# Expert bias loads in a transformer kernel: their own tiles in the first block's pool, on SyncE's queue behind the first weights of the output projection, and the down biases by GpSimd

## The chip, the cores and the metric

The kernel runs on one core of a Trainium2 chip. The time is device microseconds of one execution, and the time before is the median of three runs: 1835.69 us (1834.64 to 1837.01). The profile is one more execution, of 1836.42 us, whose instructions span 1834.6 us.

## The reference, cut to what matters

The program is a stack of two transformer blocks for 256 tokens of width 1024 (256 more tokens serve as context), all in float32. The first block ends in a mixture of 32 experts, the second in a plain network. The part around the change is the end of the first block's attention, the router, and the experts, which have biases on all three projections:

```python
mix_x = jnp.concatenate([att_x, four_x], axis=-1) @ w_out[l]
x = x + g1 * rms_norm(mix_x, norm_attn_post[l])
hx2 = modulate(x, norm_ffn_pre[l], sh2, sc2)
# moe(hx2): the router picks 4 of 32 experts for each token
logits = jnp.dot(h, w_router) + b_router
top_logit, top_idx = lax.top_k(logits, TOP_K)
...
g = jnp.minimum(xb @ w_gate[e] + b_gate[e], SWIGLU_LIMIT)
u = jnp.clip(xb @ w_up[e] + b_up[e], -SWIGLU_LIMIT, SWIGLU_LIMIT)
act = g * jax.nn.sigmoid(SWIGLU_ALPHA * g) * (u + 1)
return act @ w_down[e] + b_down[e]
```

The biases `b_gate`, `b_up` and `b_down` are 32 rows of 1024 numbers each. The weights of each expert are 12 MB, 384 MB for all of them.

## The kernel before

**Stages.** The first block is written as `pre_project` (modulation and the input projection), `pre_attend` (attention), `pre_finish` (the rest of the output projection, the residual, the router's logits and the first ranks), `route` and `experts`. The second block follows. Instructions stand in each engine's queue in the order in which the code issues them, and each queue is worked off in that order.

**The weight stream.** All large weights come through one list of jobs (`Stream`), 1 MB a tile, issued by SyncE's queue (SP) at line 161 into five rings of buffers of 7, 6, 3, 2 and 3 tiles. `pump` issues the next job as soon as its ring has a free place in the program's order; on the chip the issue waits for the buffer's last reader. Some jobs carry small loads that are issued with them (the table `also`, line 394). For the output projection four tiles `w_out` come in the order 3, 0, 1, 2; ACT and DVE split each into a high and a low part (lines 1564 and 1565) that live in ring 1, which then serves the first tiles of the experts. The 21 first expert tiles fill all five rings: expert 0's gate and up, expert 1's gate (8 + 4 tiles), expert 1's up (4), expert 0's down (4) and one tile more. Ring 3 opens when the attention's pool closes, ring 4 when all of `pre_finish` is done.

**Semaphores of the transfers.** Transfers issued by SP and ACT signal on eight semaphores, DMAHW0 to DMAHW7, one for each transfer in turn. Before a semaphore is used again the issuing queue waits for the transfer that used it last. The waits stand in the order shown below in brackets.

**The end of the output projection.** `out_part(i)` (line 361 for its matmuls) adds part i of eight to four banks: token tile 0 in banks 0 and 1, token tile 1 in banks 2 and 3. Its last call issues parts 6 and 7 bank after bank, six matmuls each. After each call one small job of the list `fills` (line 866) is issued: the gain row, the router's bias and weights, the bias rows of the second block (line 1695), then `expert_bias_in`, which issues eight loads from ACT's queue (`b_gate` and `b_up` in two halves each, lines 957, and `b_down` in four pieces, line 960), and `bias_split`, in which ACT casts the raw biases (line 968) and DVE subtracts (line 971). The raw tiles `braw` take over two places of the pool B, by the tags `mrow` and `uT`; `mrow` holds the second block's bias table until then, and `uT` a part of the keys.

**The tail.** `gained` squares the two banks of a token tile on ACT (line 888) and scales them on DVE (line 890); `added` makes the root mean square and adds to `x` (lines 894 to 899); `turned` transposes `x` on TensorE (line 905) and copies it (line 906), and `logits` multiplies by the router's weights (line 916). An Exp table is loaded (line 928), the ranks are made (lines 1007 and 1008) and the expert stage begins with the gather of tokens (line 1291) and the first gate matmul (line 1208). `warm` issues matmuls whose results nobody reads.

Of the kernel before, what the change touches and what calls it, by code (L numbers as in the profile page):

```python
# [9 lines left out]
F32 = mybir.dt.float32  # L10
# [9 lines left out]
P = 128  # L20
D = 1024
KD = 8
T = 256
E = 32
# [15 lines left out]
QMOD, KVA, SMALL, QA, EARLY = 1, 3, 0, 2, 3  # L40
# [178 lines left out]
class Kernel:  # L219
# [143 lines left out]
    def pre_project(self, A, B):  # L363
        tc, nc, I = self.tc, self.nc, self.I
# [7 lines left out]
        for nm, n in rows:  # L372
            src = I[nm]
            if len(src.shape) == 2:
# [15 lines left out]
        kp = lambda a: a.rearrange("(k p) f -> p k f", p=P)  # L390
# [1 line left out]
        nc.sync.dma_start(out=x, in_=tp(I["x"][0]))  # L392
        nc.sync.dma_start(out=xc, in_=tp(I["ctx"][0]))
        also = {("i", 3): [(pc, I["pre"]), (self.wf, I["w_fourier"][0].rearrange("(i g) c d -> (g c) i d", g=2))],
                ("q", 2): [(self.wr, kp(I["w_router"][0])), (self.br, I["b_router"])], ("k", SMALL): self.post_small()}

        def add(nm, q, cols, f, split=None):
            st.add(cols, lambda v: f(v) + also.get((nm, q), []), 0, split)
# [1 line left out]
        for q in range(4):  # L400
            for i in (1, 0):
                o = D * i + 256 * q
# [49 lines left out]
        b = self.bank()  # L452
# [77 lines left out]
        for k in range(KD):  # L530
            if k % 2 == 0:
                w = st.get()
            h = (hi[k // 4][:, k % 4], lo[k // 2][:, k % 2])
# [15 lines left out]
            else:  # L549
                st.prepare(EARLY)  # L550
                b = self.bank("vr", "m")
# [298 lines left out]
    def pre_finish(self, B, C, R):  # L850

        nc, st = self.nc, self.stream
        mod, bo = self.mod, self.bo
        gu = B.tile([P, 2048], F32, tag="sqk", name="gu")
        g1b = gu[:, 0:D]

        def router():

            b = self.bank("lb", "s")
            for k in range(KD):  # L860
                nc.tensor.matmul(b[:, 0:E], mod[:, 0, 24 + k : 25 + k].to_broadcast([P, P]), self.wr[:, k], start=(k == 0), stop=False)
            nc.tensor.matmul(b[:, 0:E], self.c("ones", 1), self.br, start=False, stop=True)
            nc.vector.tensor_copy(self.lbias, b[:, 0:E])
            nc.vector.tensor_tensor(self.wr, self.wr, self.a2.unsqueeze(2).to_broadcast([P, KD, E]), OP.mult)

        fills = [lambda: self.bcast_row(C, self.gc, g1b, bank="b"), router, lambda: self.bias_rows(B), lambda: self.expert_bias_in(B, R),
                 lambda: self.bias_split(R)]

        for i in range(2, KD):
            self.out_part(i)  # L870
            if fills:
                fills.pop(0)()

        x, ident = self.x, self.c("ident")
        ss = C.tile([P, 2], F32, name="ss2")

        self.sd = R.tile([P, 2], F32, name="sd")
        self.r2 = R.tile([P, 2], F32, name="r2")
        xT = B.tile([P, 2048], F32, tag="pc", name="x1T").rearrange("p (k t) -> p k t", k=KD)
        self.logits = {}  # L880

        s2 = [C.tile([P, 4], F32, name=f"s2{t}") for t in range(2)]
        us = {}

        def gained(t):
            for n in range(2):
                jk = C.tile([P, 512], F32, tag="prob", name="jk", bufs=3)
                nc.scalar.activation(jk, bo[2 * t + n], AF.Square, accum_out=s2[t][:, n : n + 1])
                u = us[t, n] = B.tile([P, 512], F32, tag=("mrow", "uT")[n], name="u") if t else gu[:, D + 512 * n : D + 512 * n + 512]
                nc.vector.tensor_tensor(u, bo[2 * t + n], g1b[:, 512 * n : 512 * n + 512], OP.mult)  # L890

        def added(t):
            s = s2[t]
            nc.vector.tensor_tensor(s[:, 2:3], s[:, 0:1], s[:, 1:2], OP.add)
            nc.scalar.activation(s[:, 3:4], s[:, 2:3], AF.Sqrt, bias=self.eps[1e-6], scale=1.0 / D)
            nc.vector.reciprocal(s[:, 3:4], s[:, 3:4])
            for n in range(2):
                o = x[:, t, 512 * n : 512 * n + 512]
                nc.vector.scalar_tensor_tensor(o, us[t, n], s[:, 3:4], o, OP.mult, OP.add)

        def turned(t):
            for h in range(2):
                b = self.bank()
                for k in range(4):
                    nc.tensor.transpose(b[:, k * P : (k + 1) * P], x[:, t, (4 * h + k) * P : (4 * h + k + 1) * P], ident)
                nc.scalar.copy(xT[:, 4 * h : 4 * h + 4, t * P : (t + 1) * P], b.rearrange("p (k t) -> p k t", k=4))

        def norm(t):
            r = self.sd[:, t : t + 1]
            nc.scalar.activation(gu[:, 0:D] if t else B.tile([P, D], F32, tag="lk0", name="jk2"), x[:, t], AF.Square, accum_out=ss[:, t : t + 1])  # L910
            nc.scalar.activation(r, ss[:, t : t + 1], AF.Sqrt, bias=self.eps[1e-6], scale=1.0 / D)

        def logits(t):
            self.logits[t] = self.bank("lb", "o")[:, 0:E]
            for k in range(KD):
                nc.tensor.matmul(self.logits[t], xT[:, k, t * P : (t + 1) * P], self.wr[:, k], start=(k == 0), stop=(k == KD - 1))

        self.route_open(R)
        gained(0)
        added(0)  # L920
        gained(1)
        turned(0)
        added(1)
        norm(0)
        logits(0)
        turned(1)
        norm(1)
        nc.scalar.activation(ss[:, 0:1], self.eps[1e-6], AF.Exp)
        self.choose(0)
        logits(1)  # L930
        self.ranks_of(0)
        self.choose(1)
        self.warm(WARM2)
        self.ranks_of(1)
        self.warm(WARM3)
        self.dump("x1", x)
# [9 lines left out]
            self.moe_end(M)  # L946
        self.held.close()

    def expert_bias_in(self, B, R):


        self.braw = {}
        for nm, tag in (("b_gate", "mrow"), ("b_up", "uT")):
            t = self.braw[nm] = B.tile([P, 512], F32, tag=tag, name="braw")
            b = self.I[nm]
            for h in range(2):
                self.nc.scalar.dma_start(out=t[64 * h : 64 * h + 64], in_=bass.AP(tensor=b.tensor, offset=b.offset + 512 * h, ap=[[0, 2], [D, E], [1, 512]]))
        self.bdn = R.tile([P, T], F32, name="bdn")
        for q in range(4):
            self.nc.scalar.dma_start(out=self.bdn[E * q : E * q + E], in_=self.I["b_down"][0][:, T * q : T * q + T])  # L960

    def bias_split(self, R):

# [1542 lines left out]
```

## Time and profile before

| what | value |
|---|---|
| median of three runs | 1835.69 us |
| the profiled execution | 1836.42 us, span 1834.6 us |
| TensorE busy, share of the span | 1732.3 us, 94% |
| VectorE / ScalarE / GpSimd busy | 752.9 / 589.9 / 57.9 us |
| bytes moved | 553.45 MB, mean 302 GB/s |
| mean granted TensorE clock | 0.983 of full |

The page draws the span in 40 slices of 45.9 us. In slices 7 to 25 (from 275 us to 1147 us) the transfers run at 410 to 413 GB/s: that is the expert stage. Before it the rates lie between 197 and 405 GB/s, and the granted clock is below 9 tenths in the third and the fifth slice: these stages are made of short steps that wait for each other. After it the second block has TensorE busy in 9 tenths of nearly every slice and the transfers at 23 to 249 GB/s. Times in the text are microseconds from the span's start.

### The profile page before, as it was taken

The numbers are of one execution on the slowest core, as the hardware profiler recorded it, in microseconds if no ns is written. First come the engines' busy times: TensorE is split into PE (matmuls) and PEld (weight loads), VectorE is DVE, ScalarE is ACT, GpSimd is POOL, SyncE is SP. The second block draws the span as 40 slices with busy tenths as digits, with TensorE's granted clock in tenths as the row PEclk, the third lists the DMA queues.
The fourth block names the chain that finished last, engine by engine and source line by source line (L and its number), as shares of the span: only waits on it lengthen the run. The fifth ranks groups of instructions, "written<-read, shape, count | busy, mean of one in ns | idle before, by whom it ended". The sixth has DMA issues, their size and how long they took to land. (4 is left out here: it accounts for less than half of the span.)

```text
span 1834.6 us, 24464 instructions
## 1 busy us (share of the span) xinstructions
PE 1732.3 (94%) x9537; PEld 1038.8 (57%) x9537; DVE 752.9 (41%) x1582; ACT 589.9 (32%) x1158; POOL 57.9 (3%) x52
## 2 busy tenths in 40 slices
PE   7889599999999989999989988899999999999998
PEld 6756553333333323333323332388689989989997
DVE  4786242222222212222211211476675558756555
ACT  4544221111111101111111110355654445555444
POOL 0340000000000000000000000100000001000000
PEclk9989799999999999999999999999999999999999
DMA  9767599999999999999999999987245554435540
GB/s 350 262 242 265 197 356 405 412 412 411 410 412 413 412 412 412 410 411 412 412 413 412 413 411 411 338 249 230 70 161 186 185 188 154 132 116 203 185 158 23
DMA packets 202525, 553.45 MB, mean 302 GB/s; under 512 B 11136, under 2 KB 87558, under 8 KB 200358
## 3 DMA queue, kind: packets, MB, share of 16 engines
q1 hardware_dynamic: 201026, 549.82, 79.4%
q8 instruction: 76, 1.25, 0.3%
q10 hardware_dynamic: 932, 1.29, 0.2%
q0 software_dynamic: 448, 0.73, 0.1%
q14 instruction: 43, 0.35, 0.1%
HBM read 550.71 MB, written 1.07 MB: 301 GB/s over the span
## 5 line engine op out<-in xcount | busy, mean ns | idle before, releaser
L1565 DVE TENSOR_TENSOR ring<-ring,ring 128x1024 fp32r<-128x1024 f32 x196 | 230.6, 1221 | 78.2 <-ACT ring L1564 77.6
L1208 PE MATMUL g<-ring,xg 128*64 128x512 f32 x1056 | 254.0, 603 | 8.1 <-DMA ring<-in_w_gate 8.1
L1208 PE MATMUL u<-ring,xg 128*64 128x512 f32 x1056 | 248.2, 602 | 10.7 <-DMA ring<-in_w_up 9.7
L1219 PE MATMUL y<-ring,ht 128*64 128x512 f32 x1056 | 241.1, 599 | 15.9 <-DMA ring<-in_w_down 15.4
L1564 ACT CAST ring<-ring 128x1024 fp32r<-128x1024 f32 x196 | 195.3, 1049 | 75.7 <-PE acc L1794 54.3
L1280 ACT ACTIVATE z<-y,gsl 64x512 fp32r<-64x512 f32 x66 | 45.0, 682 | 428.6 <-PE y L1219 401.6
L1779 PE MATMUL ot<-ahi,ring 128*128 128x256 f32 x960 | 177.2, 282 | 0.0
L1219 PEld LDWEIGHTS y<-ring,ht 128*64 128x64 f32 x1056 | 69.9, 136 | 164.6 <-issue 117.6
L1281 DVE SCALAR_TENSOR_TENSOR z<-y,gsl,z 64x512 fp32r<-64x512 f32 x66 | 49.5, 750 | 250.6 <-ACT z L1280 250.5
L1779 PEld LDWEIGHTS ot<-ahi,ring 128*128 128x128 f32 x960 | 151.3, 191 | 1.3
L1208 PEld LDWEIGHTS u<-ring,xg 128*64 128x64 f32 x1056 | 67.3, 136 | 132.5 <-issue 98.9
L1208 PEld LDWEIGHTS g<-ring,xg 128*64 128x64 f32 x1056 | 66.9, 136 | 126.9 <-issue 118.7
L1779 PE MATMUL ot<-alo,ring 128*128 128x256 f32 x480 | 135.6, 283 | 0.0
L1794 PE MATMUL acc<-ring,hhi 128*128 128x512 f32 x480 | 131.5, 395 | 0.0
L1794 PEld LDWEIGHTS acc<-ring,hhi 128*128 128x128 f32 x480 | 88.1, 188 | 19.0
L1227 ACT ACTIVATE sg<-gm 128x512 f32<-128x512 f32 x33 | 20.8, 630 | 238.8 <-DVE gm L1226 238.8
L1779 PEld LDWEIGHTS ot<-alo,ring 128*128 128x128 f32 x480 | 91.8, 191 | 1.3
L1293 ACT ACTIVATE xg<-xg,mod,a 128x128 f32<-128x128 f32 (+1 forms) x136 | 50.9, 452 | 98.3 <-PE xg L1291 98.3
L1779 PE MATMUL pj<-ahi,ring 128*128 128x256 f32 x416 | 80.0, 287 | 0.0
L1291 PEld LDWEIGHTS xg<-pm,x 128*128 128x128 f32 x544 | 63.7, 191 | 26.2 <-issue 14.6
L1270 DVE TENSOR_SCALAR gt<-gt,cp 128x256 fp32r<-128x256 f32 x33 | 16.0, 484 | 150.4 <-PE gt L1268 150.4
L1794 PE MATMUL acc<-ring,hlo 128*128 128x512 f32 x240 | 75.4, 395 | 0.0
(520 smaller groups left out, 2157.2 us busy)
## 6 DMA issues: line engine op xcount, KB each, us to landing
ring<-in_w_gate SPq DMA_DIRECT2D x128, 1024.0 KB, 18.1
ring<-in_w_up SPq DMA_DIRECT2D x128, 1024.0 KB, 18.1
ring<-in_w_down SPq DMA_DIRECT2D x128, 1024.0 KB, 18.1
ring<-in_mlp_w SPq DMA_DIRECT2D x64, 1024.0 KB, 5.3
ring<-in_w_mod SPq DMA_DIRECT2D x24, 1024.0 KB, 7.0
ring<-in_odd_w_in SPq DMA_DIRECT2D x12, 1024.0 KB, 5.7
ring<-in_even_w_in SPq DMA_DIRECT2D x7, 1024.0 KB
ring<-in_w_out SPq DMA_DIRECT2D x4, 1024.0 KB, 5.4
```

The costliest lines, as they stand in the source:

```text
L1208: nc.tensor.matmul(acc[64 * h : 64 * h + 64], xg[:, 2 * q + j], w[:, j, 512 * h : 512 * h + 512], start=(q == 0 and j == 0), stop=False, s ...
L1219: nc.tensor.matmul(acc[64 * h : 64 * h + 64], l, w[:, j, 512 * h : 512 * h + 512], start=(q == 0 and j == 0), stop=(q == 3 and j == 1), sk ...
L1227: nc.scalar.activation(sg, gm, AF.Sigmoid, scale=1.702)
L1270: nc.vector.tensor_scalar(gt, b, self.c("misc")[:, 0:1], None, OP.is_equal)
L1280: nc.scalar.mul(t[s], a[s], g[s])
L1281: nc.vector.scalar_tensor_tensor(t[o], a[s], g[s], t[s].bitcast(F32), OP.mult, OP.subtract)
L1291: nc.tensor.matmul(b[:, n * j : n * j + n], self.x[:, t, (k + j) * P : (k + j + 1) * P], pm[:, t, 0:n], start=(t == 0), stop=(t == 1))
L1293: nc.scalar.activation(xg[:, k + j], b[:, n * j : n * j + n], AF.Identity, bias=self.mod[:, 0, 24 + k + j : 25 + k + j], scale=self.a2[:, ...
L1564: nc.scalar.copy(hi[:, c], v[:, c])
L1565: nc.vector.tensor_tensor(lo[:, c], v[:, c], hi[:, c].bitcast(F32), OP.subtract)
L1779: nc.tensor.matmul(out, w[a][:, k, c : c + n], x[b][:, k], start=(k == 0 and i == 0), stop=(k == KD - 1 and i == 2))
L1794: nc.tensor.matmul(acc[2 * t + n], x[a][kx][:, t * P : (t + 1) * P], w[b][:, j, 512 * n : 512 * n + 512], start=(first and i == 0), stop=( ...
```

## The change

The raw gate and up biases get tiles of their own in pool B, which no other tile shares, and their four loads are appended to the job of the first `w_out` tile, so SP issues them. The four loads of the down biases stay in the list of fills, but are issued by GpSimd instead of ACT.

```diff
                 ("q", 2): [(self.wr, kp(I["w_router"][0])), (self.br, I["b_router"])], ("k", SMALL): self.post_small(),
+                ("o", 3): self.expert_bias_in(B)}
...
-        fills = [..., lambda: self.bias_rows(B), lambda: self.expert_bias_in(B, R),
+        fills = [..., lambda: self.bias_rows(B), lambda: self.down_bias_in(R),
                  lambda: self.bias_split(R)]
...
-    def expert_bias_in(self, B, R):
+    def expert_bias_in(self, B):
         self.braw = {}
-        for nm, tag in (("b_gate", "mrow"), ("b_up", "uT")):
-            t = self.braw[nm] = B.tile([P, 512], F32, tag=tag, name="braw")
+        loads = []
+        for nm in ("b_gate", "b_up"):
+            t = self.braw[nm] = B.tile([P, 512], F32, name=f"{nm}r")
             b = self.I[nm]
             for h in range(2):
-                self.nc.scalar.dma_start(out=t[64 * h : 64 * h + 64], in_=bass.AP(..., ap=[[0, 2], [D, E], [1, 512]]))
+                loads.append((t[64 * h : 64 * h + 64], bass.AP(..., ap=[[0, 2], [D, E], [1, 512]])))
+        return loads
+
+    def down_bias_in(self, R):
         self.bdn = R.tile([P, T], F32, name="bdn")
         for q in range(4):
-            self.nc.scalar.dma_start(out=self.bdn[E * q : E * q + E], in_=self.I["b_down"][0][:, T * q : T * q + T])
+            self.nc.gpsimd.dma_start(out=self.bdn[E * q : E * q + E], in_=self.I["b_down"][0][:, T * q : T * q + T])
```

**ACT's queue at the end of the output projection, before** (`bkt` is the second block's bias rows, `braw` the raw biases, `bdn` the down biases, `jk,s<-mix` the first square of the tail):

```order
L1695 ACTIVATE bkt<-bk 16x384 [waits PE_49]
L957 DMA braw<-in_b_gate 64x1x512 [waits DMAHW7_49,DMAHW3_49]
L957 DMA braw<-in_b_gate 64x1x512 [waits DMAHW4_49]
L957 DMA braw<-in_b_up 64x1x512 [waits DMAHW6_49]
L957 DMA braw<-in_b_up 64x1x512
L960 DMA bdn<-in_b_down 32x256 [waits DMAHW0_49,DVE_49,Activation_49]
L960 DMA bdn<-in_b_down 32x256 [waits DMAHW1_49]
L960 DMA bdn<-in_b_down 32x256 [waits DMAHW2_49]
L960 DMA bdn<-in_b_down 32x256 [waits DMAHW4_49]
L968 CAST b_gate<-braw 128x512 [waits DMAHW3_49]
L968 CAST b_up<-braw 128x512 [waits DMAHW7_49,DMAHW6_49]
L888 ACTIVATE jk,s_1678<-mix 128x512 [waits PE_49]
```

The same place with the change (`b_gater` and `b_upr` are the raw biases):

```order
L1700 ACTIVATE bkt<-bk 16x384 [waits PE_49]
L973 CAST b_gate<-b_gater 128x512 [waits DMAHW4_49,DMAHW5_49,DVE_49,Activation_49]
L973 CAST b_up<-b_upr 128x512 [waits DMAHW7_49,DMAHW6_49]
L889 ACTIVATE jk,s_1678<-mix 128x512 [waits PE_49]
L889 ACTIVATE jk,s_1678<-mix 128x512 [waits DVE_49,PE_49]
L896 ACTIVATE s_1678<-s_1678,eps_72 128x1 [waits DVE_49]
```

The eight loads are gone from ACT; the two casts stand directly behind `bkt` and wait for semaphores of loads that SP issues.

**SP's queue at the `w_out` tiles, before:**

```order
L161 DMA ring_1111<-in_w_mod 128x2048 [waits DMAHW2_49,DVE_49,Pool_49]
L161 DMA ring_1117<-in_w_out 128x2x1024 [waits DMAHW4_49,PE_49]
L161 DMA ring_1168<-in_w_out 128x2x1024 [waits DMAHW5_49,PE_49]
L161 DMA ring_1209<-in_w_out 128x2x1024 [waits DMAHW6_49,PE_49]
L161 DMA ring_1215<-in_w_out 128x2x1024 [waits DMAHW7_49,PE_49]
```

The same place with the change:

```order
L161 DMA ring_1113<-in_w_mod 128x2048 [waits DMAHW2_49,DVE_49,Pool_49]
L161 DMA ring_1119<-in_w_out 128x2x1024 [waits DMAHW4_49,PE_49]
L161 DMA b_gater<-in_b_gate 64x1x512
L161 DMA b_gater<-in_b_gate 64x1x512 [waits DMAHW5_49]
L161 DMA b_upr<-in_b_up 64x1x512 [waits DMAHW6_49]
L161 DMA b_upr<-in_b_up 64x1x512 [waits DMAHW7_49]
L161 DMA ring_1174<-in_w_out 128x2x1024 [waits DMAHW0_49,PE_49]
L161 DMA ring_1215<-in_w_out 128x2x1024 [waits DMAHW1_49,PE_49]
L161 DMA ring_1221<-in_w_out 128x2x1024 [waits DMAHW2_49,PE_49]
```

Four small loads come between the first and the second `w_out` tile, and every later transfer of SP has another semaphore than before.

**SP's queue where ring 3 opens (expert 1's last two gate tiles), before:** the four up tiles and two down tiles behind them go into ring 1, the last row into ring 4.

```order
L161 DMA ring_1527<-in_w_gate 128x2x1024 [waits DMASW4_49,DMASW3_49,DMASW5_49,DMASW2_49,DMAHW2_49,DMASW1_49,DMASW0_49]
L161 DMA ring_1529<-in_w_gate 128x2x1024 [waits DMAHW5_49]
L161 DMA ring_1578<-in_w_up 128x2x1024 [waits DMAHW3_49,PE_49]
L161 DMA ring_1580<-in_w_up 128x2x1024 [waits DMAHW5_49,PE_49]
L161 DMA ring_1623<-in_w_up 128x2x1024 [waits DMAHW6_49,PE_49]
L161 DMA ring_1625<-in_w_up 128x2x1024 [waits DMAHW7_49,PE_49]
L161 DMA ring_1670<-in_w_down 128x2x1024 [waits DMAHW0_49,PE_49]
L161 DMA ring_1672<-in_w_down 128x2x1024 [waits DMAHW1_49,PE_49]
L161 DMA ring_1797<-in_w_down 128x2x1024 [waits DMASW6_49,DMAHW2_49,DVE_49,DMAHW4_49,PE_49,Activation_49]
```

The same place with the change:

```order
L161 DMA ring_1533<-in_w_gate 128x2x1024 [waits DMASW3_49,DMASW2_49,DMASW4_49,DMASW1_49,DMASW5_49,DMASW0_49,DMAHW6_49,PE_49,Activation_49]
L161 DMA ring_1535<-in_w_gate 128x2x1024 [waits DMAHW7_49]
L161 DMA ring_1584<-in_w_up 128x2x1024 [waits DMAHW0_49,PE_49]
L161 DMA ring_1586<-in_w_up 128x2x1024 [waits DMAHW1_49,PE_49]
L161 DMA ring_1629<-in_w_up 128x2x1024 [waits DMAHW2_49,PE_49]
L161 DMA ring_1631<-in_w_up 128x2x1024 [waits DMAHW3_49,PE_49]
L161 DMA ring_1670<-in_w_down 128x2x1024 [waits DMAHW4_49,PE_49]
L161 DMA ring_1672<-in_w_down 128x2x1024 [waits DMAHW5_49,PE_49]
L161 DMA ring_1797<-in_w_down 128x2x1024 [waits DMASW6_49,DVE_49,DMAHW6_49,PE_49,Activation_49]
```

Before, the up tiles share DMAHW3, DMAHW6 and DMAHW7 with the bias loads of ACT, and the down tiles DMAHW0 and DMAHW1 with the down biases; now they share theirs with weight tiles and one small load of ACT. The tile that opens ring 3 waits for PE and Activation as well.

## Rows read from the trace of the kernel before

**Rows 1.** Windows: busy us (instructions) by engine, granted clock, DMA share, GB/s.

```profile
180.00:200.00 20.00, 19.31 (x87) 14.20 (x85) 1.90 (x10) 1.65 (x3) 0.56 (x1) 1.00 0.57 214
200.00:220.00 20.00, 1.68 (x8) 1.57 (x8) 6.84 (x13) 4.40 (x12) 0.00 (x0) 0.56 0.72 249
220.00:230.00 10.00, 10.00 (x46) 9.61 (x45) 3.89 (x16) 6.14 (x13) 0.78 (x1) 0.50 0.29 114
...
1000.00:1150.00 150.00, 133.31 (x594) 45.79 (x593) 28.23 (x56) 18.48 (x36) 0.00 (x0) 1.00 1.03 411
```

**Rows 2.** Timeline of ScalarE: start, us, instruction, idle before it and releaser.

```profile
191.20 0.48 ACT L1695 ACTIVATE bkt<-bk 16x384 f32<-16x384 f32 x1 [7.88 <-PE bk L1693]
191.26 1.24 ACTq L957 DMA_DIRECT2D braw<-in_b_gate  x2
...
193.90 6.32 ACTq L960 DMA_DIRECT2D bdn<-in_b_down  x4
200.26 0.62 ACT L968 CAST b_gate<-braw 128x512 fp32r<-128x512 f32 x1 [8.58 <-DMA braw<-in_b_gate]
213.46 0.62 ACT L968 CAST b_up<-braw 128x512 fp32r<-128x512 f32 x1 [12.58 <-DMA braw<-in_b_up]
213.98 0.59 ACT L888 ACTIVATE jk<-mix 128x512 f32<-128x512 f32 x1
...
214.56 0.59 ACT L888 ACTIVATE jk<-mix 128x512 f32<-128x512 f32 x1
```

**Rows 3.** Timeline of TensorE, from the output projection to the first expert matmul.

```profile
185.27 1.87 PE L861 MATMUL lb<-wr,mod 128*128 128x32 f32 x16
...
191.09 8.46 PE L361 MATMUL mix<-ring,mix 128*128 128x512 f32 x36
218.32 1.94 PE L905 MATMUL bk<-cp,x 128*128 128x128 f32 x8 [18.77 <-DVE x L899]
220.08 3.62 PE L916 MATMUL lb<-wr,x1T 128*128 128x32 f32 x16
...
236.14 1.94 PE L1208 MATMUL g<-ring,xg 128*64 128x512 f32 x8
```

**Rows 4.** Windows of 1 us: clock, DMA share and GB/s stand last.

```profile
202.00:203.00 1.00, 0.00 (x0) 0.00 (x0) 0.29 (x1) 0.00 (x0) 0.00 (x0) 0.69 1.02 342
211.00:212.00 1.00, 0.00 (x0) 0.00 (x0) 0.00 (x0) 0.00 (x0) 0.00 (x0) 0.50 0.12 49
...
233.00:234.00 1.00, 1.00 (x7) 0.82 (x7) 0.66 (x4) 0.00 (x0) 0.00 (x0) 0.95 1.05 430
```

**Rows 5.** Waits of SP's queue, 120 to 270 us: total, times, longest.

```profile
SPq L161 <- DMA braw<-in_b_gate: 17.6, 1, 17.6
SPq L161 <- DMA braw<-in_b_up: 15.3, 2, 7.9
```

**Rows 6.** Timeline of SP's issues, merged.

```profile
125.19 0.89 SPq L161 DMA_DIRECT2D ring<-in_w_out  x2
...
196.77 17.04 SPq L161 DMA_DIRECT2D ring<-in_w_up  x4
...
229.00 0.88 SPq L161 DMA_DIRECT2D ring<-in_w_down  x2
```

**Rows 7.** Timeline, two steps of the tail.

```profile
217.42 1.42 DVE L899 SCALAR_TENSOR_TENSOR x<-gu,s,x 128x512 f32<-128x512 f32 x2
...
228.78 0.20 ACT L928 ACTIVATE ss<-eps 128x1 f32<-128x1 f32 x1
```

**Rows 8.** Timeline of ScalarE: the splits of the second and the fourth `w_out` tile.

```profile
162.38 2.01 ACT L1564 CAST ring<-ring 128x1024 fp32r<-128x1024 f32 x2
...
174.11 1.99 ACT L1564 CAST ring<-ring 128x1024 fp32r<-128x1024 f32 x2 [2.23 <-PE mix L361]
```

**Rows 9.** Landing of the `w_out` tiles (median us), and the first use of the down biases.

```profile
ring<-in_w_out SPq DMA_DIRECT2D x4, 1024.0 KB, 5.4
...
L1377 DVE COPY bdw<-bdn x4: 282/284/290, 360.5 to 368.3; 32x256 f32<-32x256 f32 x4
```

More of the change, by code (lines that the diff above doesn't have):

```diff
@@ L394, in pre_project @@
         also = {("i", 3): [(pc, I["pre"]), (self.wf, I["w_fourier"][0].rearrange("(i g) c d -> (g c) i d", g=2))],
-                ("q", 2): [(self.wr, kp(I["w_router"][0])), (self.br, I["b_router"])], ("k", SMALL): self.post_small()}
+                ("q", 2): [(self.wr, kp(I["w_router"][0])), (self.br, I["b_router"])], ("k", SMALL): self.post_small(),
+                ("o", 3): self.expert_bias_in(B)}
         def add(nm, q, cols, f, split=None):
@@ L864, in router @@
             nc.vector.tensor_tensor(self.wr, self.wr, self.a2.unsqueeze(2).to_broadcast([P, KD, E]), OP.mult)
-        fills = [lambda: self.bcast_row(C, self.gc, g1b, bank="b"), router, lambda: self.bias_rows(B), lambda: self.expert_bias_in(B, R),
+        fills = [lambda: self.bcast_row(C, self.gc, g1b, bank="b"), router, lambda: self.bias_rows(B), lambda: self.down_bias_in(R),
                  lambda: self.bias_split(R)]
@@ L947, in moe @@
         self.held.close()
-    def expert_bias_in(self, B, R):
+    def expert_bias_in(self, B):
         self.braw = {}
-        for nm, tag in (("b_gate", "mrow"), ("b_up", "uT")):
-            t = self.braw[nm] = B.tile([P, 512], F32, tag=tag, name="braw")
+        loads = []
+        for nm in ("b_gate", "b_up"):
+            t = self.braw[nm] = B.tile([P, 512], F32, name=f"{nm}r")
             b = self.I[nm]
             for h in range(2):
-                self.nc.scalar.dma_start(out=t[64 * h : 64 * h + 64], in_=bass.AP(tensor=b.tensor, offset=b.offset + 512 * h, ap=[[0, 2], [D, E], [1, 512]]))
+                loads.append((t[64 * h : 64 * h + 64], bass.AP(tensor=b.tensor, offset=b.offset + 512 * h, ap=[[0, 2], [D, E], [1, 512]])))
+        return loads
+    def down_bias_in(self, R):
         self.bdn = R.tile([P, T], F32, name="bdn")
         for q in range(4):
-            self.nc.scalar.dma_start(out=self.bdn[E * q : E * q + E], in_=self.I["b_down"][0][:, T * q : T * q + T])
+            self.nc.gpsimd.dma_start(out=self.bdn[E * q : E * q + E], in_=self.I["b_down"][0][:, T * q : T * q + T])
     def bias_split(self, R):
```

## The prediction

> **What bounds the kernel now.** I read the windows by stage first, then the timelines of the stage that stood out, then the waits.
>
> In the expert stage the transfers run at 411 GB/s without a pause and TensorE has work for 133 of 150 us [rows 1]: the length of that stage is the length of its transfers, so it ends earlier only if the stream starts earlier. What starts it is TensorE: at the head of the stage every ring is full, and a new tile is asked for when a buffer is read out. The stage of interest lies ahead of it. From 180 to 200 us TensorE is busy for 19.3 us, from 200 to 220 for 1.7 us [rows 1]. The last matmul of the output projection ends at 191.09 + 8.46 = 199.55 us and the next one starts at 218.32, after 18.77 us of idleness [rows 3].
>
> Nobody computes in that gap. ACT has issued the eight bias loads and then waits: 8.58 us for `b_gate`, 12.58 us for `b_up` [rows 2]. Its two casts stand ahead of the tail's first square, so that square starts at 213.98 us, though its four banks were done by 199.55. TensorE's wait is put down to DVE's `x`, which is the end of the same chain.
>
> The loads also hold up the weight stream, because they share semaphores with it: SP waits 17.6 us for `b_gate` and 15.3 us for `b_up` [rows 5], and the four up tiles of expert 1 are issued over 17.04 us from 196.77 on [rows 6]. Ring 4's first tile goes out at 229.00 [rows 6], just behind ACT's Exp step, which ends at 228.98 [rows 7]; the transfer engines are busy for only 0.29 of 220 to 230 us [rows 1].
>
> **The change part by part.**
>
> *The loads leave ACT.* Now the casts follow `bkt`, which ends at 191.68, and take 2 x 0.62 us [rows 2]: ACT is free at 192.9, beside the mix matmuls, if the raw biases have landed. DVE's four subtractions fit beside them too: DVE is busy 1.9 of 20 us there [rows 1].
>
> *The restart of TensorE.* A mix matmul takes 8.46 / 36 = 0.235 us [rows 3]. The last 24 go bank by bank, six each, so the banks are done at 195.3, 196.7, 198.1 and 199.55, and the order rows of the change show a PE wait of its own on each square. The second square can start at 196.7, where it started at 214.56 before [rows 2]. From that square to the first transpose it took 218.32 - 214.56 = 3.76 us [rows 2, 3]; the same distance puts the transposes at 200.5. That is 17.8 us earlier, with 0.9 us of idleness in place of 18.8.
>
> *From the restart to the first expert matmul* it took 236.14 - 218.32 = 17.8 us [rows 3], nearly all of it at half clock: the granted clock fell at about 202.4 (0.69 is the mean of the microsecond from 202, with 1.00 before and 0.50 after), 3 us after TensorE fell idle, and came back at 233 [rows 4]. It stayed at 0.50 through 220 to 230, where TensorE counts as busy for all 10 us [rows 1]; there it does transposes and matmuls of 32 columns. Those are slow at that level: 16 matmuls of 32 columns take 3.62 us, and 1.87 us among the mix matmuls at full clock [rows 3]. With the change TensorE enters this tail at 2.4 GHz. Since the same work did not bring the clock back, I take it that it doesn't hold it either, and that it falls again some 3 us into the tail. Then the first transposes (1.94 us at half clock, about half of it saved) and the first logits (3.62 - 1.87 = 1.75 saved) run fast: 2.7 us less, of which I count 2.2, because ACT's copies between them keep their length. Bounds: 0 (half clock all along) and about 4.7 (full clock all along: the second transposes and logits save the same 2.7 once more, but the second token tile also waits for DVE and ACT).
>
> *The stream behind it.* The bias loads no longer hold any semaphore of the up and down tiles, so each goes out when its buffer is free: the first two up tiles after part 3 of the projection, so before the last 36 mix matmuls begin at 191.09, the next two after 12 of these, at about 194, the two down tiles at 199.6. All land before ring 4 opens. Ring 4 opens behind the Exp step, whose distance to the first expert matmul stays about the same (236.14 - 229.00 = 7.1 us), so the stream starts earlier by what TensorE gains. From there on both run as before.
>
> *The four loads on SP's queue.* Their cost is what they do to the three `w_out` tiles behind them. In their old place the four and the down biases needed from 191.26 to 213.46 = 22.2 us [rows 2], sharing with weights; that is the upper bound. The lower one: while only bias traffic was left it ran at 49 GB/s [rows 4], and 4 x 128 KB at that rate is 10.7 us. SP spends four issues of 0.62 us [rows 2] = 2.5 us more. The first two `w_out` tiles went out within 125.19 + 0.89 us, the second at about 125.7 [rows 6]; with 2.5 of issue, 22.2 of bias traffic and 5.4 of landing [rows 9] it is there at 155.8, and its split starts at 162.38 [rows 8]: 6.6 us to spare. The last two follow in the same queue at 1.05 MB / 411 GB/s = 2.55 us each, by 161, and the fourth one's split starts at 174.11 [rows 8]. So I take 0, hidden under the attention's last steps; if that cover were gone, each further microsecond would cost one. A gain is excluded, since nobody waits for these tiles now.
>
> The row of 49 GB/s shows a DMA share of 0.12, two engines of sixteen [rows 4]. The Trainium skill (DMA: Bandwidth & Descriptors, on why a DMA increments its semaphore by 16 and not by 1) says why: a load is spread over the largest number of engines, up to 16, that divides the slowest dimension of both sides, and here the source's slowest dimension is 2. The row agrees. It speaks against the new place, since all four loads queue on the same two engines, with the `w_out` pieces of these engines behind them; by it the tiles come 10.7 us later, inside the bounds above, and the sum doesn't change.
>
> *The down biases on GpSimd.* Their four issues took ACT 6.32 us with their waits [rows 2]; GpSimd has 0.56 us of work in that window [rows 1], so they end there near 200 us, and the first reader comes at 360.5 [rows 9]. Bounds 0 and 0 on the path; below nothing only what ACT gains, which is counted.
>
> *Sum.* 17.8 + 2.2 = 20.0 us. The profiled execution took 1836.42 us, so it becomes 1816.4; it stood 0.73 above the median, and from the median I forecast 1815.7 us.
>
> **The rivals.**
>
> *The clock holds through the tail.* 17.8 + 4.7 = 22.5 us, 1813.2 us. For it: the pauses in the tail are now below 1 us. Against: ten microseconds of this same work left the clock at 0.50 [rows 1].
>
> *Half clock all along.* 17.8 us, 1817.9 us, if the clock is already down when the tail starts.
>
> *The squares wait for the whole projection.* Then the tail starts at 199.6 instead of 213.98: 14.4 us, 1821.3 us. Against it: each square has its own bank.
>
> *SP gets stuck where ring 3 opens.* In the order of the change that tile waits for PE and Activation too, since the pools have moved by the new tiles. If these waits last only to the end of the attention, about 180 us, they cost nothing: the tiles behind can't go before their own buffers are free. If they last to the last mix matmul, eight tiles go out from 199.6 on, at 2.55 us each to 220.0, and ring 4's three to 227.7, where they took from 229.00 to 236.7 before: 9 us, 1827 us. Against it: the ring takes the attention's place, and the projection's operands lie in another pool.
>
> *The gain is given back in the expert stage*: 1835.7 us. For it: its tiles are prefetched, and 21 MB lie ready in either case. Against it: the stage's rate is constant, so its end moves with its start.
>
> *Slower: the bias loads hold the output projection.* They now stand ahead of three `w_out` tiles in one queue, on two engines. The second tile's split is late from 22.2 + 6.6 = 28.8 us of bias traffic on, the change is a loss from 48.8 us on, and at 60 us the time would be 1835.7 + 11.2 = 1847 us. For it: up to 22.2 us were seen. Against it: that was with ring tiles and down biases in between, and behind the `w_mod` tiles little else competes.
>
> **How the numbers follow.** Forecast with the falling clock 0.48 (own range 1814 to 1817.5); clock holds 0.22; half clock all along 0.08; late squares 0.06; ring 3 stuck 0.05; given back 0.05; slower 0.04; the remaining 0.02 are other gains. The range 1811.8 to 1820.0 takes in the first three and the uncertainty of their sums, and leaves out about 0.2. A measurement of this kernel can tell 0.2%, 3.7 us, from no change: every case but the last two is faster by more, 0.91; same 0.05; slower 0.04.
>
> **What would show it.** In the profile after: ACT's casts at about 192 us with no idle time before them; the first square before 196 us; the transposes of `x` at 199.6 to 200.6; ring 4's first tile at about 209; the first gate matmul at about 216; the granted clock falling once around 203 to 204 and back before 216. The split of the second `w_out` tile still at 162.4 shows the loads' new place to be free; a wait there for `w_out` or SP stuck before 200 us shows it wrong. An expert stage that starts 20 us earlier but ends less than 18 us earlier would refute the step on the stream.

## The result, and the profile after

The changed kernel takes 1813.16 us (median of three runs, 1811.28 to 1815.61); the ratio to the kernel before is 0.9882, with an interval of 0.9861 to 0.9903. That is 22.5 us less; 20.0 were forecast. The profiled execution took 1811.28 us, with a span of 1809.5.

The windows of the kernel after, in the columns of [rows 1]:

```profile
180.00:200.00 20.00, 19.69 (x102) 15.50 (x101) 8.13 (x17) 7.05 (x17) 2.54 (x5) 1.00 0.97 366
200.00:220.00 20.00, 18.48 (x121) 12.56 (x122) 11.70 (x65) 10.00 (x24) 1.89 (x2) 1.00 0.90 342
220.00:230.00 10.00, 10.00 (x47) 3.13 (x43) 3.89 (x13) 1.30 (x3) 0.00 (x0) 1.00 0.99 377
...
1000.00:1150.00 150.00, 135.08 (x600) 46.27 (x600) 26.85 (x54) 20.53 (x39) 0.00 (x0) 1.00 1.02 407
```

The hole from 200 to 220 us is closed (18.48 us busy in place of 1.68), and the granted clock, third column from the end, reads 1.00 throughout, where [rows 1] has 0.56 and 0.50. The expert stage runs as before.

The timeline of ScalarE (ACT), which answers to [rows 2]:

```profile
189.03 0.60 ACT L973 CAST b_gate<-b_gater 128x512 fp32r<-128x512 f32 x1
189.53 0.62 ACT L973 CAST b_up<-b_upr 128x512 fp32r<-128x512 f32 x1
192.95 0.60 ACT L889 ACTIVATE jk<-mix 128x512 f32<-128x512 f32 x1 [2.80 <-PE mix L361]
...
194.31 0.60 ACT L889 ACTIVATE jk<-mix 128x512 f32<-128x512 f32 x1 [0.67 <-PE mix L361]
```

The casts no longer wait for a DMA, and each square waits only for its own bank of the projection.

The timeline of TensorE (PE), which answers to [rows 3]:

```profile
187.79 0.81 PE L1698 MATMUL bk<-bk,relb 33*16 33x384 f32 x2
188.53 8.46 PE L361 MATMUL mix<-ring,mix 128*128 128x512 f32 x36
197.25 1.29 PE L906 MATMUL bk<-cp,x 128*128 128x128 f32 x8 [0.26 <-DVE x L900]
198.55 1.97 PE L917 MATMUL lb<-wr,x1T 128*128 128x32 f32 x16
...
210.66 1.94 PE L1213 MATMUL g<-ring,xg 128*64 128x512 f32 x8
```

The pause ahead of the tail is 0.26 us in place of 18.77, and the first logits take 1.97 us in place of 3.62.

The 36 matmuls start at 188.53 here and at 191.09 in [rows 3]. These 2.56 us are not the change's: they come before its place, and over all kernels run here that start lies between 186.7 and 191.1 us, in kernels with the old and with the new place alike. It goes with the granted clock far ahead of the change: from 20 to 40 us this reads 0.83 in the four profiles that start latest (190.9 to 191.1 us, before among them), 1.00 in the two that start earliest (186.7 and 186.8) and 0.91 in the other eight, after among them; what makes it differ between executions was not tried. I therefore cut each profiled execution at three points: the `relb` matmul ahead of the 36 (187.79 above; it stands 0.75 us ahead of them in every kernel), the first transpose and the first expert matmul.

```
                              to relb   relb to     transposes     from there    median   ratio to before
                                        transposes  to experts     to the end
before                        190.34    27.98       17.82          1598.5        1835.69
after                         187.79     9.46       13.41          1598.8        1813.16  0.9882
down biases on ACT again      185.94     9.46       13.42          1598.2        1812.52  0.988
down biases moved alone       187.51    33.13       18.40          1599.0        1840.60  1.0026
after, ACT busy long          186.27    26.61       17.83          1599.9        1835.09  0.9995
after, ACT busy short         188.84    12.73       18.40          1600.7        1819.94  0.9918
 again                        190.15    12.73       18.46          1599.2        1820.47  0.992
 with the pause filled        190.30    12.74       13.80          1599.1        1816.37  0.9891
before, spread loads          186.05    12.96       18.36          1599.1        1818.12  0.9913
 and down biases on GpSimd    187.60    13.56       18.05          1599.3        1820.28  0.9917
after, bias loads doubled     187.57     9.46       13.40          1599.2        1813.08  0.9888
after, spread loads           188.75     9.46       13.41          1601.1        1812.48  0.9873
before, 68 warming matmuls    190.34    28.35       17.38          1600.8        1838.76  1.0021
before, 86 warming matmuls    189.00    28.47       13.84          1597.8        1832.93  1.0
```

From before to after the second column gives 18.52 us and the third 4.41, together 22.9; with the 2.55 of the first and the -0.4 of the last it is the 25.1 us by which the spans differ.

Three more pieces of after. SP's issues, in order:

```profile
122.75 0.39 SPq L161 DMA_DIRECT2D ring<-in_w_out  x1
123.20 1.24 SPq L161 DMA_DIRECT2D b_gater<-in_b_gate  x2
124.48 5.45 SPq L161 DMA_DIRECT2D b_upr<-in_b_up  x2
130.04 5.06 SPq L161 DMA_DIRECT2D ring<-in_w_out  x3
...
205.32 0.88 SPq L161 DMA_DIRECT2D ring<-in_w_down  x2
```

The last three `w_out` tiles go out behind the four loads; ring 4's first tile goes out at 205.32, where it was 229.00 [rows 6]. Of SP's waits from 120 to 250 us, the one that is left of ring 3's opening:

```profile
SPq L161 <- ACT mx L828: 1.5, 1, 1.5
```

And the splits of the second and fourth `w_out` tile, which answer to [rows 8]:

```profile
159.80 2.01 ACT L1569 CAST ring<-ring 128x1024 fp32r<-128x1024 f32 x2
...
171.53 1.99 ACT L1569 CAST ring<-ring 128x1024 fp32r<-128x1024 f32 x2 [2.23 <-PE mix L361]
```

Both stand where they stood, less the 2.6 us, and neither waits for a load (the 2.23 us are a wait for a matmul, as before).

### The profile page after: what moved, and what is told of

Same layout as the page of the kernel before. It is cut to its first block, busy times and chain, and to the rows that moved or that the text cites. A ratio compares the mean times of both kernels' runs of the same rounds, so it can differ in the third digit from the quotient of the medians.

```text
span 1809.5 us, 24471 instructions
## 1 busy us (share of the span) xinstructions
PE 1725.8 (95%) x9537; PEld 1031.7 (57%) x9537; DVE 752.8 (42%) x1582; ACT 590.5 (33%) x1158; POOL 60.0 (3%) x56
```

## The experiments

Theory A: the gain is ACT, which no longer waits ahead of the tail's squares, and what TensorE's clock does for having no pause. Theory B: the gain is SP's stream, which no longer waits on semaphores that it shared with the bias loads. Each experiment's profiled execution is a row of the table above.

**One part of the change alone.** The loads of the gate and up biases moved, the down biases left on ACT:

```
-  self.nc.gpsimd.dma_start(out=self.bdn[...], in_=self.I["b_down"]...)
+  self.nc.scalar.dma_start(out=self.bdn[...], in_=self.I["b_down"]...)
```

> The changed kernel, but the four loads of the down biases stay in ACT's queue. Theory A (what pays is that ACT no longer waits ahead of the tail's squares): ACT spends at most the 6.3 us of those four issues ahead of the casts, so the second square comes some 3 to 4 us later than in the changed kernel: about 1817 us, and the rest of the gain stays. Theory B (what pays is that SP's weight tiles no longer share semaphores with the bias loads): the down biases share two or more of them again, but they are short and early enough: 1813 us. A third reading, that the move of the down biases to GpSimd is the larger part, gives 1825 us or more.

Measured 1812.52 us, ratio 0.988 (0.9863 to 0.9896): the whole gain. ACT's issues of the down biases in this kernel:

```profile
186.88 1.74 ACTq L965 DMA_DIRECT2D bdn<-in_b_down  x4
```

They took 6.32 us in [rows 2], with their queue full of other loads; behind nothing they take 1.74, beside the matmuls. So that move is worth nothing here, and A's price for it, 3 to 4 us, was wrong: these issues end before the squares could start. Between A and B this run does not decide. Now the other part alone, the down biases on GpSimd and the rest as before:

> The kernel before, with only the four loads of the down biases moved to GpSimd; the raw gate and up biases keep their old places and ACT's queue. Theory A: ACT still waits for both halves of b_up, which land at most a few us sooner without the down biases beside them: 1831 to 1836 us. Theory B: SP still waits for the semaphores of b_gate and b_up (17.6 and 15.3 us): 1833 to 1836 us. The third reading (the down biases are the larger part): 1822 us or less.

Measured 1840.60 us, ratio 1.0026 (1.0015 to 1.0037): a little slower, where every theory expected the same time or less. The casts, in its timeline of ACT:

```profile
201.93 0.62 ACT L968 CAST b_gate<-braw 128x512 fp32r<-128x512 f32 x1 [13.09 <-DMA braw<-in_b_gate]
215.78 0.62 ACT L968 CAST b_up<-braw 128x512 fp32r<-128x512 f32 x1 [13.23 <-DMA braw<-in_b_up]
```

They wait 5.2 us longer than in [rows 2], with fewer loads on the queue. SP asked for the up tiles from 182.41 us on, where it was held until 196.77 in [rows 6], and these tiles fill the transfer engines while the bias loads run. The window behind it, with share and GB/s last:

```profile
190.00:200.00 10.00, 6.72 (x30) 5.24 (x28) 0.00 (x0) 0.00 (x0) 1.91 (x4) 0.97 0.90 269
```

The kernel before moved 97 GB/s there at a share of 0.31 (191 to 200 us). That the tiles delay the loads is read from these rows and was not tried by itself.

**ACT kept busy in the changed kernel.** Everything as in the change, SP's stream included, but ACT copies a raw bias tile onto itself 30 times behind the casts:

```
+        for _ in range(30):
+            nc.scalar.mul(self.braw["b_gate"], self.braw["b_gate"], 1.0)
```

> The changed kernel, with 30 copies of a 128x512 tile onto itself on ACT (0.6 us each, 18 us) between the casts and the tail's first square. The weight stream keeps its new freedom. Theory A: the squares start near 209 us instead of 193, TensorE is idle for some 14 us, its clock falls as it did before, and the time goes back to 1813 + 15 + 4.7 = about 1833 us. Theory B: the tiles are asked for early all the same, so nearly the whole gain stays: 1813 to 1817 us.

Measured 1835.09 us, ratio 0.9995 (0.9985 to 1.0005): the whole gain is gone. ACT's copies and TensorE's restart:

```profile
189.64 19.82 ACT L978 ACTIVATE b_gater<-b_gater 128x512 f32<-128x512 f32 x30 [1.00 <-DVE b_gate L976]
```

```profile
212.88 1.94 PE L906 MATMUL bk<-cp,x 128*128 128x128 f32 x8 [17.41 <-DVE x L900]
```

B expected 1813 and falls. SP asks for the four up tiles just as early, 5.1 us ahead of `relb` in both kernels; here is that row of after, then of this one:

```profile
182.68 9.55 SPq L161 DMA_DIRECT2D ring<-in_w_up  x4
```

```profile
181.16 9.55 SPq L161 DMA_DIRECT2D ring<-in_w_up  x4
```

The stream up to ring 4 is the same, and the pause is back. With nine copies instead of 30:

> The changed kernel with nine copies of 0.66 us on ACT behind the casts, so that ACT is free at about 195.6 instead of 192.9 and TensorE restarts about 2 us later, behind a pause of 2 us. Theory A (the order on ACT ahead of the squares): 1814 to 1816 us if the clock holds over such a pause, 1818 to 1820 if it falls. Theory B (SP's stream): no change, 1813 us.

Measured 1819.94 us, ratio 0.9918 (0.9899 to 0.9937). Only 3.27 us are lost up to the transposes, but 5.0 in the tail behind them, at half clock. This leaves the question whether a pause of 3.5 us alone does that.

**The clock by itself.** The same kernel again, and beside it one with 14 warming matmuls (`self.warm(7)`) behind the projection, which fill that pause and change nothing else:

> The short ACT block again, on the same chip as its twin with the pause filled, so that the two are compared directly: 1818 to 1822 us by every theory, tail 18.4 us at half clock.

> The kernel of the short ACT block (nine copies, 3.5 us of pause ahead of the tail, clock at half through the tail, 1819.9 us) with 14 warming matmuls, 3.05 us, behind the projection, so that the same pause is filled. Theory of the clock (the tail keeps 2.4 GHz when TensorE enters it without a pause, worth 4.4 to 5 us): first gate matmul 13.4 us behind the first transpose instead of 18.4, total 1814 to 1816 us. Rival (what ACT's late squares cost is not the clock): 1819 to 1821 us.

Measured on one chip: 1820.47 us with the pause, ratio 0.992 (0.9906 to 0.9933), and 1816.37 with the pause filled, ratio 0.9891 (0.9876 to 0.9906). TensorE with the pause:

```profile
202.88 1.94 PE L906 MATMUL bk<-cp,x 128*128 128x128 f32 x8 [3.54 <-DVE x L900]
204.65 3.62 PE L917 MATMUL lb<-wr,x1T 128*128 128x32 f32 x16
...
221.34 1.94 PE L1215 MATMUL g<-ring,xg 128*64 128x512 f32 x8
```

and with the pause filled:

```profile
199.34 3.18 PE L268 MATMUL warm<-cp 128*128 128x256 f32 x14
203.04 1.29 PE L907 MATMUL bk<-cp,x 128*128 128x128 f32 x8 [0.51 <-DVE x L901]
204.34 1.97 PE L918 MATMUL lb<-wr,x1T 128*128 128x32 f32 x16
...
216.84 1.94 PE L1216 MATMUL g<-ring,xg 128*64 128x512 f32 x8
```

The first transposes start at the same distance from `relb` (12.73 and 12.74 us), and the tail is 4.66 us shorter. Their windows from 204 to 214 us, the first with the pause, the second with it filled:

```profile
204.00:214.00 10.00, 10.00 (x47) 9.55 (x46) 3.92 (x14) 6.69 (x13) 0.23 (x1) 0.50 0.22 88
```

```profile
204.00:214.00 10.00, 8.38 (x60) 7.14 (x57) 7.40 (x30) 6.41 (x13) 1.59 (x2) 1.00 0.47 153
```

At 0.50 (1.2 GHz) TensorE counts as busy all the time and does 47 matmuls; at 1.00 (2.4 GHz) it does 60 in less. The medians differ by 4.1 us, and no execution of the one kernel reaches into the range of the other (1819.78 to 1822.57 us, 1813.56 to 1817.67): that is the size of the clock term.

**Warming matmuls in the kernel before**, behind the projection, to bridge the wait for the loads. First 68 of them (`self.warm(34)`), then 86 (`self.warm(43)`):

> The kernel before, with 34 matmuls of 256 columns whose results nobody reads, behind the last part of the output projection: at full clock they fill some 17.5 of TensorE's 18.8 idle us. Nothing else is changed, so only the granted clock in the tail can move the time. If TensorE's clock is the second term of the gain (4.7 us as reckoned, tail at full clock): 1831 us, with the clock at 1.00 from 200 to 236 us. If the tail itself lets the clock fall, as the forecast took: 1833 to 1834 us. If the clock is no term: 1835.7 us.

Measured 1838.76 us, ratio 1.0021 (1.0009 to 1.0033). The warming matmuls ended 4.5 us too early:

```profile
199.38 14.84 PE L268 MATMUL warm<-cp 128*128 128x256 f32 x68
218.69 1.68 PE L906 MATMUL bk<-cp,x 128*128 128x128 f32 x8 [4.47 <-DVE x L900]
```

The clock still read 1.00 when the transposes began and 0.50 from 220 us on, so the tail shortened by only 0.4 us. This does not test the theory, which needs the pause to be gone.

> The kernel before with 86 warming matmuls behind the projection instead of 68. They should end at about 218.2 us, half a microsecond ahead of the first transpose, where the 68 left 4.5 us of idleness and the clock fell one microsecond into the tail. Theory of the clock (entered without a pause, the tail keeps 2.4 GHz and is 4.4 us shorter): first gate matmul 13.4 us behind the first transpose instead of 17.4, total 1831 to 1832 us. Rival (the small matmuls of the tail can't hold the clock, and what held it in the changed kernel is something else): the clock falls about 3 us into the tail, 1834 to 1836 us.

Measured 1832.93 us against 1833.63 for the kernel before on that chip, ratio 1.0 (0.9989 to 1.0012). In its profiled execution the pause is 0.71 us and the tail 13.84 us, as the theory says:

```profile
217.47 1.29 PE L906 MATMUL bk<-cp,x 128*128 128x128 f32 x8 [0.71 <-DVE x L900]
...
231.31 1.94 PE L1209 MATMUL g<-ring,xg 128*64 128x512 f32 x8
```

Yet the median did not follow. The profiled execution is the fastest of the ten (1830.92 us), and its mean granted clock is the highest, 0.993; the other nine read 0.988 to 0.992, with 0.990 as the median. By an estimate from these numbers, 0.003 of 1831 us is 11 us more at half clock (0.003 x 1831 / 0.5), most of a tail's length. That suggests that the clock fell in most of the others, since the warming is of fixed length and the wait for the loads need not be. It doesn't show it: a mean over the whole execution can't say where the clock was low, and executions of the kernel before on that chip spread as much (0.983 to 0.987). So this stays open, and so does what makes the first of the two slower by 0.2%. The pair with the copies on ACT, whose pause is of fixed length, is the measurement to go by.

**The two engines.** The kernel before, its loads on ACT as they were, but as eight loads of 32 rows:

```
-  self.nc.scalar.dma_start(out=t[64*h : 64*h+64], in_=bass.AP(..., ap=[[0, 2], [D, E], [1, 512]]))
+  for r in range(2):
+      self.nc.scalar.dma_start(out=t[64*h+32*r : 64*h+32*r+32], in_=bass.AP(..., ap=[[D, E], [1, 512]]))
```

> The kernel before, its loads of the two biases still on ACT and at their old place, but as eight loads of 32 rows each instead of four of two times 32. If the wait of ACT came from the two engines that such a load keeps (rows of 49 GB/s at a share of 0.12), the loads spread over all sixteen land within some 5 us of their issue, the second cast ends before 200, the first transpose stands at 200 to 203 and the total falls by 15 to 20 us: 1816 to 1821 us, without any move. If the wait is the queue behind the weight tiles or the latency of loads as such, the casts stay near 200 and 213 and the total stays at 1833 to 1837 us.

Measured 1818.12 us, ratio 0.9913 (0.9894 to 0.9931): 15.5 us of the 22.5 without moving a load. The casts and the restart:

```profile
192.75 0.62 ACT L969 CAST b_gate<-braw 128x512 fp32r<-128x512 f32 x1 [5.37 <-DMA bdn<-in_b_down]
193.28 0.61 ACT L969 CAST b_up<-braw 128x512 fp32r<-128x512 f32 x1
```

```profile
199.01 1.94 PE L905 MATMUL bk<-cp,x 128*128 128x128 f32 x8 [3.76 <-DVE x L899]
```

Here the second cast begins 6.3 us after ACT's first issue of these loads (186.97 us), before 22.2 us [rows 2]. What is left is the pause of 3.76 us, and the clock at 0.50 behind it. Each load lands 1.9 to 2.2 us after its own issue. The Trainium skill (DMA: Bandwidth & Descriptors, on why a DMA increments its semaphore by 16 and not by 1) gives a load the largest number of engines, up to 16, that divides the slowest dimension of both sides, which is 2 for the old form and 16 for this one. The trace agrees in these landing times. The first cast seems to wait for the down biases, which were still issued on ACT until 192.71, so these were moved to GpSimd in the next kernel:

> The kernel before, the loads of the two biases at their old place on ACT but spread as eight loads of 32 rows, and the down biases on GpSimd. Against the spread loads alone (1818.1 us; the first cast waited for the issue of the down biases until 192.75, and a pause of 3.8 us was left) ACT is free some 2 us earlier. Theory (only the time at which ACT is free for the squares counts, not the queue that the loads are on): the pause falls to under 2 us, the tail keeps 2.4 GHz, 1811 to 1815 us, the whole gain of the change without a move to SP. If the landing of the loads ends last instead: no change against the spread alone, 1817 to 1820 us.

Measured 1820.28 us, ratio 0.9917 (0.9904 to 0.9931). The expected 1811 to 1815 us is refuted, and the rival's 1817 to 1820 is just passed:

```profile
190.29 4.03 ACTq L958 DMA_DIRECT2D braw<-in_b_up  x4
...
193.49 0.83 ACTq L958 DMA_DIRECT2D braw<-in_b_up  x2
...
194.83 0.62 ACT L969 CAST b_gate<-braw 128x512 fp32r<-128x512 f32 x1 [5.89 <-DMA braw<-in_b_up]
196.29 0.62 ACT L969 CAST b_up<-braw 128x512 fp32r<-128x512 f32 x1 [0.83 <-DMA braw<-in_b_up]
```

The loads themselves land last, 6 to 8 us after their first issue, among weight tiles (331 GB/s at a share of 0.97 from 190 to 194 us). Two things add up here: each load now lands 2.3 to 5.0 us after its own issue, and the last two go out only at 193.49, because ACT's queue is held after the second of the four. The pause ahead of the tail is 4.35 us in place of 3.76. Issued at this place they are late even when spread; of the kernels run, only those with the earlier place have the full gain.

**What the new place costs.** The changed kernel with its four bias loads issued twice (`return loads + loads`):

> The changed kernel with its four bias loads issued twice, so that the two engines have double the traffic ahead of the last three tiles of w_out. The prediction held 6.6 us of cover to be left over beside up to 22 us of traffic. Theory narrow cover (in the changed kernel the two engines were busy alone until about 157 us, and the second tile is split at 159.8): ten more microseconds of traffic make that split 7 to 10 us late, and the total is 1819 to 1824 us. Theory wide cover: no wait at the split, 1811 to 1815 us.

Measured 1813.08 us, ratio 0.9888 (0.9868 to 0.9908). The second four wait for the first, so that the tiles go out 11.8 us later than in after:

```profile
133.38 3.13 SPq L161 DMA_DIRECT2D b_gater<-in_b_gate  x2
138.65 3.14 SPq L161 DMA_DIRECT2D b_upr<-in_b_up  x2
141.84 4.13 SPq L161 DMA_DIRECT2D ring<-in_w_out  x3
```

The split of the second tile still begins at 159.59 us without a wait: the cover holds for twice the traffic, and the theory of a narrow cover falls. Its premise was misread, too: in after the two engines run alone only in short stretches, one of them from 158 to 162 us, and not all the way to 157. And the changed kernel with spread loads:

> The changed kernel with its bias loads as eight loads of 32 rows. The stretches at about 50 GB/s (130 to 133 us) and at about 275 GB/s with full share (136 to 144 us) go, the tiles of w_out land in some 5 us instead of 9, and since nobody waited for them the total stays at 1811 to 1814 us. Rival (the two slow engines do hold something ahead of the tail): 1808 to 1811 us.

Measured 1812.48 us, ratio 0.9873 (0.9858 to 0.9888): not to be told from after. Windows, with share and GB/s last; first two of after, then the same of this kernel:

```profile
138.00:140.00 2.00, 2.00 (x9) 1.60 (x9) 1.25 (x4) 0.62 (x2) 0.00 (x0) 1.00 1.05 271
158.00:160.00 2.00, 2.00 (x10) 1.37 (x9) 1.21 (x7) 1.80 (x6) 0.00 (x0) 1.00 0.12 49
```

```profile
138.00:140.00 2.00, 2.00 (x7) 1.07 (x7) 1.80 (x3) 0.18 (x1) 0.00 (x0) 1.00 1.01 414
158.00:160.00 2.00, 2.00 (x9) 1.57 (x10) 1.14 (x4) 0.79 (x3) 0.00 (x0) 1.00 0.43 176
```

The stretch at 49 GB/s from 158 us goes, and nobody had waited for it. The expectation was missed in part: of the last three `w_out` tiles one lands after 5.0 us and one after 9.1 (the third shows no landing), and from 134 to 136 us the rate still dips to 72 GB/s. No kernel here is measurably faster than after.

## Why the prediction was right, and where it was not

*The loads leave ACT:* right. The casts follow `bkt` without a wait, and when ACT is kept busy instead, the whole gain goes.

*The restart of TensorE:* right, 18.5 us measured for 17.8 forecast. The rest is the distance from the second square to the transposes, counted as 3.76 us from the row of before and now 197.25 - 194.31 = 2.94. The 0.82 us lie in DVE's scaling of the two banks: before, `b_up`'s subtractions held it until 215.49, and it was through with both banks 2.23 us after the second square had started; now the first bank is done by then, and it takes 1.41.

*The clock term:* the step that failed, in its mechanism and so in its size. The prediction had it that the tail's small matmuls do not hold the clock because they did not bring it back, and counted 2.2 us; the clock stayed at 1.00 through the tail, and the term is 4.4 us in the profile and 4.1 between the medians of the pair. Keeping the clock and getting it back are not the same: the work that ran ten microseconds at 0.50 in [rows 1] without a rise ran at 1.00 here without a fall, with a longest pause of 1.35 us:

```profile
206.86 0.41 PE L1013 MATMUL ranks<-mask,cp 128*128 128x32 f32 x2 [1.35 <-DVE mask L1006]
```

This rival (1813.2 us, chance 0.22) is the case that came, and the forecast missed it by the 2.5 us between the two. The range held both, so the time alone would have hidden the error; the clock in the profile and the pair with the copies on ACT show it. Part of the near agreement with 1813.2 is luck: 0.7 us more at the restart, 0.3 less at the clock and 0.4 less at the end nearly cancel. What in the work lets the clock stay but not return was not tried.

*The stream behind it:* right. From the first expert matmul to the end every kernel takes 1598 to 1601 us, whatever came before; nothing is given back.

*The four loads on SP's queue:* right at 0, since even doubled traffic met no waiting reader, but not by the sum as it stands. Four issues were counted at 2.5 us, and SP spent 6.7 on them (123.20 to 129.93): the two of `b_up` took 2.9 and 2.5 each, and by the order rows they wait for semaphores of earlier transfers. The second `w_out` tile went out at 130.04, where it had gone out at 125.67 (123.1 with the 2.6 us taken off). The last one was hardly delayed: it went out at 133.9, and at 136.1 before, so it did not follow the second closely even then. The landing of 5.4 us [rows 9] is that of the third tile alone, the only one of the four for which the profile before gives a landing. The slower rival had its price from this cover and falls with it.

*The down biases on GpSimd:* costed at nothing, which is right, and worth nothing either.

*Half clock all along, late squares, SP stuck:* the clock at 1.00, squares bank by bank, and a wait of 1.5 us refute them.

Of the signs named, the casts, the squares and the transposes came where they were put once the 2.6 us of the earlier start are taken off. On the same footing ring 4's first tile came at 207.9 instead of 209 and the first gate matmul at 213.2 instead of 216, both early; the fall of the clock did not come.

## What to carry to other kernels

A load that an in-order engine consumes ahead of work others wait for costs that wait, and then the clock behind the pause: count both. Ask first how many transfer engines the load uses, since a change of its shape gave two thirds of this gain without a move. Don't infer from rows at 1.2 GHz whether the same work keeps 2.4 GHz; look for a row of it at that level.

## What the runs showed of the hardware that was not expected

In the fourteen profiles the tail takes one of two lengths: 13.4 to 13.8 us where TensorE entered it from matmuls with a pause of 0.26 to 0.71 us, and 17.4 to 18.5 behind pauses of 3.5 us and more. Nothing in between was seen.

Behind the bias loads of two engines the `w_out` tiles ran at 271 GB/s with the engines' share at 1.05, and at 414 GB/s and 1.01 behind spread ones. A full share is no full rate; why it is so was not tried.

Taking the four small loads of the down biases off ACT alone made the wait for the others longer (8.58 and 12.58 us became 13.09 and 13.23). SP got its weight tiles out earlier there (182.41 in place of 196.77); that these delayed the loads is read from the rows, not tried.
